# Head products on 64 array rows, two heads in turn, instead of zero-padded 128-row products

## The chip, the core and the metric

The kernel runs on one core of one Trainium2 chip. All numbers are 32-bit floats; the larger matrix products use pairs of a rounded and a remaining part ("hi" and "lo"), three products to one. The metric is the device time of one execution in microseconds (us).

## The reference

256 tokens of width 1024 go through two blocks, one after the other. Cut to what matters here:

```python
# first block: a mixer of two halves, then a layer of 32 experts
z = h @ w_in                                   # h: normalised, modulated x
y_a = gmlp_mixer(zu, zv, ...)
y_b = rwkv7_mixer(zr, ...)                     # 8 heads of 64 channels:
#   state = state * w[:, None, :] + (state @ a)[..., None] * b[:, None, :] + v[..., None] * k[:, None, :]
#   y_t   = state @ r
x = x + gate1 * (concatenate([y_a, y_b]) @ w_out)
x = rmsnorm(x + gate2 * hier_moe(...))
# second block: two layers
for i in range(2):
    q, k, v = heads(h @ w_qkv[i])              # 16 heads of 64 channels
    if i == 0:                                 # stick-breaking attention, s < t
        z = (q @ k.T) * 64 ** -0.5
        a = exp(log_sigmoid(z) + after)        # after: sum of log_sigmoid(-z) over s < j < t
    else:                                      # forgetting attention, s <= t
        a = softmax(z + cum_t - cum_s)
    x = x + gt_a * rmsnorm((a @ v) @ w_o[i])
    x = x + gt_f * rmsnorm(ffn(...))
```

## The kernel before, in words

A list scheduler decides the order of the instructions on each engine; every engine then runs its own list in order and waits on semaphores. All loads of weights are issued on SP's queue in program order. The stages follow each other: norm and gmlp and rwkv projections (to about 128 us of the profiled execution), the rwkv products (128 to about 200 us), the output projection, router and experts (to about 760 us), then layer 0 of the second block with stick-breaking attention (about 780 to 900 us), its feed-forward, layer 1 with forgetting attention, its feed-forward.

**The rwkv products.** The recurrence is computed in two chunks of 128 tokens. `Bt`, `Kt` (keys, scaled) and `AR` (what they are multiplied with, two kinds of 128 columns a chunk) hold channels on partitions: a pair `q` of heads fills 128 partitions, head `e` of the pair lies on `E2[e]`, rows 0 to 63 or 64 to 127. A product over one head's 64 channels is wanted. `BP` and `KP` are copies of `Bt` and `Kt` with one 128-row slab a head, in which the other head's rows are zero: POOL zeroes both at the kernel's start (L677, L678), ACT copies the head's 64 rows (L694, L699, 8 copies each), and TensorE multiplies all 128 rows (L738 for `BP`, L752 for `KP`). Each source line's matmul over 256 columns appears in the trace as two records, so the 16 matmuls of L738 are 32 records. DVE masks a head's first product into `NT` and `RB` (L741, L742), POOL makes `XT` of `NT` (L743, L744), and DVE transposes `XT` to `Y`, four heads' slabs at a time (L785). DVE masks a head's second product into `ma` (L755), and eight records a head multiply `ma` with `V` (L759, L760). Products of `Y` and `NT` (L776) start the inversion that follows, and quarters of modulation vectors (L184, on 32 array columns) are filled in between.

**Layer 0's scores.** `project` makes queries and keys of a pair of heads. ACT copies the keys into `kz`, one head at a time, the other head's rows zero (L1441, two copies of 64x256), and the queries into `kq` (L1444, one copy). POOL zeroes the two `kz` buffers at the block's start (L1296). `stick_scores` multiplies them (L1456 with 256 columns, L1457 with 128), head after head, into one PSUM bank a head. Layer 1 uses the same buffers: POOL zeroes `kq` (L1409), DVE writes a row of ones into `kz` (L1413).

```python
            for e in range(2):
                h = 2 * q + e
                r = AR[:, q].rearrange("p c x t -> p c (x t)")
                p = pmm()
                for c in range(2):
                    PE.matmul(p[:, 256 * c:256 * c + 256], BP[:, h, 128 * c:128 * c + 128], r[:, c, :], start=c == 0,
                              stop=c == 1, skip_group_check=True)
```

Of the kernel before, what the change touches and what calls it, by code (L numbers as in the profile page):

```python
# [11 lines left out]
F32 = mybir.dt.float32  # L12
# [8 lines left out]
D = 1024  # L21
# [4 lines left out]
BIG = 6                                                  # 8 KB slots beside the ring's  # L26
MORE = 2                                                 # and those that the experts add
QUAD = 4                                                 # the four experts after which crowded places have their turn
# of the experts' pieces of weights that are loaded ahead: those that go where later tiles lie, and the order of loading
EARLY = {4: "em", 5: "ay", 11: "oo", 17: "xg"}  # L30
ORDER = (0, 1, 2, 3, 6, 7, 8, 9, 10, 4, 5, 11, 12, 13, 14, 15, 16, 17)
# quarters of the modulation vectors emitted between other work
# [5 lines left out]
# row tiles of weights after which the products so far are emitted  # L38
ENDV = (1, 2, 3, 4, 6, 7)
ENDO = (0, 2, 3, 7)  # L40
# pieces of weights split ahead
# [3 lines left out]
ONACT = (1, 2, 3)                                        # row tiles of the first norm that ScalarE writes  # L45
# [3 lines left out]
# first columns of the parameters in their array  # L49
# [10 lines left out]
def block(ctx, tc, A, out, dbg=None):  # L60
# [7 lines left out]
    # 8 KB tiles of all phases; the experts' weights are staged in them too  # L68
# [5 lines left out]
    split = []                                           # the pool of the phase for parts of weights  # L74
# [12 lines left out]
    # ---------------------------------------------------------------- constants  # L87
# [5 lines left out]
    gt, ge = gte[:, 0, :], gte[:, 1, :]                  # [p, j]: j > p, j >= p  # L93
    DVE.tensor_scalar(gt, jp, 0.0, None, op0=OP.is_gt)
    DVE.tensor_scalar(ge, jp, 0.0, None, op0=OP.is_ge)
    sel = const.tile([128, 1], F32, name="sel")          # 1 at partitions 0, 32, 64, 96
# [4 lines left out]
    # ---------------------------------------------------------------- inputs  # L101
    par = const.tile([128, NPAR], F32, name="par")       # the parameters as columns
# [26 lines left out]
    # ---------------------------------------------------------------- weights  # L129
# [35 lines left out]
    # ---------------------------------------------------------------- c @ W rows  # L165
# [83 lines left out]
    # ---------------------------------------------------------------- rmsnorm pieces  # L249
# [1425 lines left out]
```

## Time and profile before

| What | Value |
|---|---|
| median of 3 runs | 1476.15 us (1474.22 to 1479.09) |
| span of the profiled execution, first to last instruction | 1477.1 us; the trace lists no time outside it |
| PE busy | 1375.0 us, 93% |
| DVE busy | 763.4 us, 52% |
| ACT busy | 572.5 us, 39% |
| POOL busy | 77.1 us, 5% |
| mean granted TensorE clock | 0.974 of full speed |

How to read what follows. A timeline row is the start in us, the length in us, engine, line, operation, output and inputs, shape, and how many records were joined (x); in brackets the idle time of the engine before it and what ended that. A row of groups gives the busy time in us and the mean in ns of one, then the idle time before. A row of windows gives the stretch, its length, and busy time with number of instructions for PE, weight loads (PEld), DVE, ACT and POOL, then granted clock (1.00 is 2.4 GHz, 0.50 is 1.2 GHz), DMA share and GB/s. A row of waits gives who waited for whom: total us, times, longest. The ends of PE's records are modelled, so starts are used.

### The profile page before, as it was taken

What the parts mean: (1) busy time and instruction counts of PE and PEld (TensorE: products, weight loads), DVE (VectorE), ACT (ScalarE), POOL (GpSimd) and SP (SyncE); (2) the same over time, 40 slices, a digit from 0 to 9 for tenths busy, and PEclk for the clock granted to TensorE, in tenths of its full rate; (3) what the DMA queues carried; (4) which work ended last, traced back from release to release, by engine and by line L of the source; (5) the groups of instructions that cost most, each with busy time, mean ns of one, the idle gap of its engine ahead of it and who ended that gap; (6) DMA issues with size and microseconds to landing.
All of it is one profiled execution on the core that took longest, in us unless ns stands there. A gap on an engine that the chain in (4) does not pass through costs nothing.

```text
span 1477.1 us, 24948 instructions
## 1 busy us (share of the span) xinstructions
PE 1375.0 (93%) x10350; PEld 1069.9 (72%) x10350; DVE 763.4 (52%) x1499; ACT 572.5 (39%) x1020; POOL 77.1 (5%) x77
## 2 busy tenths in 40 slices
PE   7989998799999988898979999999998999999997
PEld 5778877555545555454548876899997897799997
DVE  6648767321112112111136885788876575666665
ACT  3533014211111101011136774554556686654544
POOL 1003000000000000000010221100020001100000
PEclk9989999799999999999999998999999999999999
DMA  9825589699999999999996463787775434555540
GB/s 368 300 65 221 200 297 389 245 350 386 394 391 391 393 389 350 398 390 391 389 382 228 173 234 131 287 317 285 285 256 200 156 133 141 193 180 197 178 165 29
DMA packets 261575, 400.55 MB, mean 271 GB/s; under 512 B 6561, under 2 KB 215729, under 8 KB 261458
## 3 DMA queue, kind: packets, MB, share of 16 engines
q1 hardware_dynamic: 261458, 398.91, 75.0%
q8 instruction: 83, 1.36, 0.3%
q14 instruction: 34, 0.28, 0.1%
HBM read 397.82 MB, written 1.05 MB: 270 GB/s over the span
## 4 chain that ended last, share of the span: by engine, by line
PE 51%; DVE 3%; ACT 3%; DMA 2%; issue 1%; POOL 0%; POOLq 0%; DVEq 0%; SPq 0%; ACTq 0%
PE pmm L410 8%; PE pmm L411 7%; PE pmm L412 7%; PE pacc L410 5%; PE pacc L411 5%; PE pacc L412 5%; PE pmm L1191 4%; PE pmm L1214 3%; DMA wcols<-in_moe_w_up_dram 1%; PE pmm L184 1%; DMA wrows<-in_w_qkv_dram 1%; PE pmm L1162 1%; PE pmm L429 1%; PE pmm L1543 1%; PE pmm L360 1%
## 5 line engine op out<-in xcount | busy, mean ns | idle before, releaser
L410 PE MATMUL pmm<-hh,whi 128*128 128x256 f32 (+1 forms) x1040 | 295.2, 284 | 2.0 <-ACT whi L161 2.0
L412 PE MATMUL pmm<-hh,wlo 128*128 128x256 f32 (+1 forms) x1040 | 296.0, 285 | 0.2 <-DVE wlo L162 0.2
L411 PE MATMUL pmm<-hl,whi 128*128 128x256 f32 (+1 forms) x1040 | 294.6, 283 | 0.0
L1191 PE MATMUL pmm<-wcols,xg 128*64 128x256 f32 x2048 | 231.7, 380 | 6.3 <-DMA wcols<-in_moe_w_up_dram 6.3
L162 DVE TENSOR_TENSOR wlo<-wcols,whi 128x1024 fp32r<-128x1024 f32 (+1 forms) x130 | 168.5, 1301 | 97.2 <-ACT whi L161 96.8
L1191 PEld LDWEIGHTS pmm<-wcols,xg 128*64 128x64 f32 x2048 | 146.2, 137 | 85.8 <-DMA wcols<-in_moe_w_up_dram 8.9
L410 PEld LDWEIGHTS pmm<-hh,whi 128*128 128x128 f32 (+1 forms) x1040 | 196.8, 189 | 8.5 <-issue 3.6
L411 PEld LDWEIGHTS pmm<-hl,whi 128*128 128x128 f32 (+1 forms) x1040 | 196.0, 188 | 1.4
L412 PEld LDWEIGHTS pmm<-hh,wlo 128*128 128x128 f32 (+1 forms) x1040 | 196.3, 189 | 0.6 <-DVE wlo L162 0.5
L161 ACT ACTIVATE whi<-wcols 128x1024 fp32r<-128x1024 f32 (+1 forms) x130 | 136.2, 1053 | 118.0 <-PE pmm L411 91.5
L162 DVE TENSOR_TENSOR wlo<-wrows,whi 128x1024 fp32r<-128x1024 f32 x87 | 108.2, 1249 | 54.3 <-ACT whi L161 53.9
L1201 DVE TENSOR_TENSOR ay<-ay,pmm 128x512 f32<-128x512 f32 x16 | 11.0, 688 | 240.1 <-PE pmm L1191 226.4
L1214 PE MATMUL pmm<-wrows,em 128*64 128x512 f32 x512 | 124.6, 598 | 11.0 <-ACT em L1206 11.0
L161 ACT ACTIVATE whi<-wrows 128x1024 fp32r<-128x1024 f32 x87 | 91.7, 1062 | 91.0 <-PE pmm L411 46.8
L1214 PEld LDWEIGHTS pmm<-wrows,em 128*64 128x64 f32 x512 | 38.9, 136 | 75.2 <-issue 58.1
L411 PE MATMUL pacc<-wlo,ah 128*128 128x512 f32 x176 | 69.2, 393 | 0.0
L410 PE MATMUL pacc<-whi,ah 128*128 128x512 f32 x176 | 68.9, 391 | 0.0
L412 PE MATMUL pacc<-whi,al 128*128 128x512 f32 x176 | 68.6, 393 | 0.0
L1222 DVE SCALAR_TENSOR_TENSOR ay<-pmm,wsl,ga 128x512 f32<-128x512 f32 x32 | 24.0, 751 | 84.7 <-PE pmm L1214 82.7
L1198 ACT ACTIVATE ay<-pmm 128x512 f32<-128x512 f32 x16 | 9.6, 598 | 131.1 <-PE pmm L1191 131.1
L1206 ACT ACTIVATE em<-pmm 128x512 f32<-128x512 f32 x16 | 9.5, 597 | 123.4 <-PE pmm L1204 123.4
L1223 ACT ACTIVATE o<-ay 128x512 fp32r<-128x512 f32 x32 | 20.2, 632 | 80.2 <-DVE ay L1222 73.0
(521 smaller groups left out, 2215.2 us busy)
## 6 DMA issues: line engine op xcount, KB each, us to landing
wcols<-in_moe_w_gate_dram SPq DMA_DIRECT2D x64, 1024.0 KB, 12.0
wcols<-in_moe_w_up_dram SPq DMA_DIRECT2D x64, 1024.0 KB, 10.7
wrows<-in_moe_w_down_dram SPq DMA_DIRECT2D x64, 1024.0 KB, 10.7
wrows<-in_w_mod_dram SPq DMA_DIRECT2D x48, 1024.0 KB, 6.9
wcols<-in_w_ffn_gate_dram SPq DMA_DIRECT2D x22, 1024.0 KB, 5.3
wcols<-in_w_ffn_up_dram SPq DMA_DIRECT2D x22, 1024.0 KB, 7.5
wrows<-in_w_ffn_down_dram SPq DMA_DIRECT2D x22, 1024.0 KB, 5.1
wrows<-in_ada_w_dram SPq DMA_DIRECT2D x16, 1024.0 KB, 7.5
```

What stands on the lines that cost most here:

```text
L161: ACT.activation(hi, src, AF.Copy)
L162: (POOL if ahead else DVE).tensor_tensor(lo, src, hi.bitcast(F32), op=OP.subtract)
L184: PE.matmul(p[32 * g:32 * g + 32, 0:n].rearrange("p (a j) -> p a j", j=32), lhsT, groups(rhs)[:, g], start=first, stop=last, skip_group_ch ...
L360: PE.matmul(p, src[:, i, 128 * kt:128 * kt + 128], dg[i], start=True, stop=True)
L410: PE.matmul(p, a[0], b[0], start=first, stop=False, skip_group_check=True)
L411: PE.matmul(p, a[0], b[1], start=False, stop=False, skip_group_check=True)
L412: PE.matmul(p, a[1], b[0], start=False, stop=last, skip_group_check=True)
L429: PE.matmul(p[:, 128 * a:128 * a + 128], c[:, 4 * n + a:4 * n + a + 1].to_broadcast([128, 128]), ident, start=a == 0, stop=a == 3, skip_gr ...
L1191: PE.matmul(p[64 * a:64 * a + 64, 256 * n:256 * n + 256], xg[:, kt, lc(es[a])], wt[a][:, kt, :], start=n == 0 and kt == 0, stop=kt == KT - ...
L1214: PE.matmul(pd[n][64 * a:64 * a + 64, :], hT[:, f, 64 * a:64 * a + 64], wt[a][:, b, 512 * n:512 * n + 512], start=f == 0, stop=f == 3, ski ...
L1222: DVE.scalar_tensor_tensor(yf, pd[n], wsl, ga2[:, ns], op0=OP.mult, op1=OP.mult)
L1223: ACT.activation(oh[:, ns], yf, AF.Copy)
```

## The change

The two padded copies `BP` and `KP` go, with their memsets and their 16 ACT copies. A new function `of_pair` takes two PSUM banks and multiplies on the head's own 64 rows, the two heads in turn. In layer 0 the keys are copied in one piece for both heads, and the scores are taken on 64 rows, heads in turn. Layer 1 keeps its padded products, so the zeroing of `kz` moves to layer 1's setup, ahead of each `kq`. The arithmetic is the same but for the zeros. All comments of the kernel are also taken out, which shifts line numbers: L738 and L752 become L727, L741/742 L736/737, L743/744 L738/739, L755 L745, L759/760 L749/750, L785 L775, L1296 and L1409 L1398, L1413 L1402, L1456 and L1457 L1445.

```diff
-        BP, KP = b8h("BP"), b8h("KP")
-        POOL.memset(BP, 0.0)
-        POOL.memset(KP, 0.0)
...
-            for e in range(2):
-                ACT.activation(BP[E2[e], 2 * q + e, :], Bt[E2[e], q, :], AF.Copy)
...
-            for e in range(2):
-                ACT.activation(KP[E2[e], 2 * q + e, :], Kt[E2[e], q, :], AF.Copy)
...
+        def of_pair(q, src):
+
+            r = AR[:, q].rearrange("p c x t -> p c (x t)")
+            ps = [pmm(), pmm()]
+            for c in range(2):
+                for e in range(2):
+                    PE.matmul(ps[e][:, 256 * c:256 * c + 256], src[E2[e], q, 128 * c:128 * c + 128], r[E2[e], c, :],
+                              start=c == 0, stop=c == 1, skip_group_check=True)
+            return ps
...
-            for e in range(2):
+            for e, p in enumerate(of_pair(q, Bt)):
...
-        for t in kz:
-            POOL.memset(t, 0.0)
...
-                for t in kq:
+                for t in kz + kq:
                     POOL.memset(t, 0.0)
...
+                    if ly == 0:
+                        t = (kz if n == "k" else kq)[pq % 2][:, 0, :]
+                        ACT.activation(t, p[:, 0:S], AF.Copy, scale=1.0 if n == "k" else HD ** -0.5)
...
-                for e in range(2):
-                    PE.matmul(pz[e][:, 0:256], z1[:, e, 0:128], mv, start=True, stop=True, skip_group_check=True)
-                    PE.matmul(pz[e][:, 256:384], z1[:, e, 128:256], mv[:, 128:256], start=False, stop=True,
-                              skip_group_check=True)
+                for o, r, t in ((slice(0, 256), slice(0, 128), slice(0, 256)),
+                                (slice(256, 384), slice(128, 256), slice(128, 256))):
+                    for e in range(2):
+                        PE.matmul(pz[e][:, o], z1[E2[e], 0, r], mv[E2[e], 0, t], start=r.start == 0, stop=True,
+                                  skip_group_check=True)
```

DVE's list in the rwkv products, before, from the mask of the eighth head's first product on (`ma` is a masked second product, `Y<-XT` a transpose of four heads' slabs):

```order
L741 TENSOR_TENSOR NT<-pmm,gte 128x2x128
L742 TENSOR_TENSOR RB<-pmm,gte 128x2x128
L785 STREAM_TRANSPOSE Y<-XT 128x512
L755 TENSOR_TENSOR ma<-pmm,gte 128x512 x3
L785 STREAM_TRANSPOSE Y<-XT 128x512 x3
L755 TENSOR_TENSOR ma<-pmm,gte 128x512 x5
```

The same place of DVE's list in the changed kernel, from the sixth head's mask on:

```order
L736 TENSOR_TENSOR NT<-pmm,gte 128x2x128
L737 TENSOR_TENSOR RB<-pmm,gte 128x2x128
L775 STREAM_TRANSPOSE Y<-XT 128x512
L736 TENSOR_TENSOR NT<-pmm,gte 128x2x128
L737 TENSOR_TENSOR RB<-pmm,gte 128x2x128
L736 TENSOR_TENSOR NT<-pmm,gte 128x2x128
L737 TENSOR_TENSOR RB<-pmm,gte 128x2x128
L745 TENSOR_TENSOR ma<-pmm,gte 128x512 x2
L775 STREAM_TRANSPOSE Y<-XT 128x512 x2
L745 TENSOR_TENSOR ma<-pmm,gte 128x512 x2
L775 STREAM_TRANSPOSE Y<-XT 128x512
L745 TENSOR_TENSOR ma<-pmm,gte 128x512 x4
```

The first transpose moved ahead of the last two heads' masks, and the second ahead of the third `ma`.

TensorE's list around layer 0's score products, before, at the fourth pair of heads (`hi` and `lo` are the next products' factors, `lb` the weights of the pair before):

```order
L1543 MATMUL pmm<-lb,vs 64x256 x2
L1545 MATMUL pmm<-lb,vs 64x128 x2
L184 MATMUL pmm<-wrows,csil 32x256 x8
L1456 MATMUL pacc<-kq_6097,kz_6095 128x256
L1457 MATMUL pacc<-kq_6097,kz_6095 128x128
L1456 MATMUL pacc<-kq_6097,kz_6095 128x256
L1457 MATMUL pacc<-kq_6097,kz_6095 128x128
L1480 MATMUL pacc<-hi,lt 128x512
```

And in the changed kernel, at the fifth pair:

```order
L1531 MATMUL pmm<-lb,vs 64x256 x2
L1533 MATMUL pmm<-lb,vs 64x128 x2
L184 MATMUL pmm<-wrows,csil 32x256 x8
L1445 MATMUL pacc<-kq_6076,kz_6074 128x256 x2
L1445 MATMUL pacc<-kq_6076,kz_6074 128x128 x2
L1468 MATMUL pacc<-hi,lt 128x512
```

The two heads' products of one size now stand next to each other; what is ahead of them and behind them is the same. In five of the eight pairs L184 stands ahead of the scores, in three (the first, second and fourth) the projections do.

## Rows read from the trace of the kernel before

**Rows 1.** The page: the chain that ended last, by engine.

```profile
PE 51%; DVE 3%; ACT 3%; DMA 2%; issue 1%; POOL 0%; POOLq 0%; DVEq 0%; SPq 0%; ACTq 0%
```

**Rows 2.** Windows: end of the rwkv products, ten us of layer 0's attention.

```profile
142.00:152.00 10.00, 8.31 (x60) 7.28 (x58) 5.50 (x9) 0.17 (x1) 0.00 (x0) 1.00 0.00 0
841.00:851.00 10.00, 10.00 (x89) 8.78 (x88) 8.13 (x16) 7.77 (x13) 2.08 (x1) 1.00 0.76 281
```

**Rows 3.** Groups by line and form, 0 to 480 us.

```profile
L785 DVE STREAM_TRANSPOSE Y<-XT 128x512 f32<-128x512 f32 x20 | 13.4, 691 | 3.4 <-POOL XT L744 3.3
L738 PE MATMUL pmm<-AR,BP 128*128 128x256 f32 x32 | 7.1, 379 | 0.0
L743 POOL TENSOR_TENSOR XT<-NT,offT 128x256 f32<-128x256 f32 x8 | 5.8, 728 | 124.0 <-DVE NT L741 124.0
L694 ACT ACTIVATE BP<-Bt 64x256 f32<-64x256 f32 x8 | 3.3, 418 | 4.4 <-DVE Bt L692 4.3
```

**Rows 4.** Timeline of the rwkv products.

```profile
129.84 0.73 POOL L743 TENSOR_TENSOR XT<-NT,offT 128x256 f32<-128x256 f32 x1 [123.99 <-DVE NT L741]
...
141.09 0.73 POOL L744 TENSOR_TENSOR XT<-XT,ident 128x256 f32<-128x256 f32 x1
...
144.38 0.43 PE L759 MATMUL pacc<-V,ma 128*128 128x64 f32 x2 [1.69 <-DVE ma L755]
...
146.22 1.51 PE L752 MATMUL pmm<-AR,KP 128*128 128x256 f32 x6
...
152.89 0.42 PE L184 MATMUL pacc<-wrows,par 128*32 128x256 f32 x4
```

**Rows 5.** Timeline: a pair's score products in layer 0.

```profile
811.35 0.70 PE L1456 MATMUL pacc<-kq,kz 128*128 128x256 f32 x2
...
812.68 0.36 PE L412 MATMUL pmm<-hh,wlo 128*128 128x256 f32 x1
```

**Rows 6.** Timeline: products on 64 and 32 array columns, then on 128.

```profile
826.10 0.65 PE L1543 MATMUL pmm<-lb,vs 128*64 128x256 f32 x4
...
826.90 1.07 PE L184 MATMUL pmm<-wrows,csil 128*32 128x256 f32 x16
...
827.90 0.39 PE L410 MATMUL pmm<-hh,whi 128*128 128x256 f32 x1
...
828.12 0.28 PE L411 MATMUL pmm<-hl,whi 128*128 128x256 f32 x1
...
828.25 0.28 PE L412 MATMUL pmm<-hh,wlo 128*128 128x256 f32 x1
```

**Rows 7.** Timeline of the norm ahead of layer 0.

```profile
766.05 3.26 DVE L1280 TENSOR_SCALAR lt<-jp 128x128 fp32r<-128x128 f32 x1
...
768.23 0.99 POOL L1296 MEMSET kz<- 128x512 f32 x2
768.31 1.07 DVE L1282 CAST one<-ones 128x128 fp32r<-128x128 f32 x1
...
771.80 1.19 PE L360 MATMUL pmm<-dg,tf 128*128 128x128 f32 x4 [7.54 <-DVE dg L1265]
```

**Rows 8.** Timeline: the last pair of layer 0.

```profile
880.36 0.53 POOL L1409 MEMSET kq<- 128x512 f32 x1 [1.97 <-PE pacc L1457]
...
884.42 2.34 POOL L162 TENSOR_TENSOR hilo<-wcols,hilo 128x1024 fp32r<-128x1024 f32 x1 [3.54 <-ACT hilo L161]
884.48 2.57 DVE L1469 TENSOR_TENSOR gm<-gm,gte 128x256 f32<-128x256 f32 x1
...
886.97 0.41 DVE L1470 TENSOR_TENSOR lb<-lb,mask 128x256 f32<-128x256 f32 x1
```

**Rows 9.** Windows: a long and a short stretch at half clock.

```profile
256.30:273.40 17.10, 8.07 (x38) 7.85 (x38) 11.61 (x45) 3.68 (x7) 4.68 (x2) 0.50 0.69 230
...
925.30:928.70 3.40, 3.32 (x16) 3.05 (x16) 1.25 (x3) 2.19 (x5) 0.64 (x1) 0.50 1.00 408
```

**Rows 10.** PE's waits over the whole run.

```profile
PE pmm L381 <- ACT ga L224: 1.9, 1, 1.9
```

More of the change, by code (lines that the diff above doesn't have):

```diff
@@ L673, in block @@
         Bt, Kt, km = qt("Bt"), qt("Kt"), qt("km")
-        b8h = lambda n: b8(n).rearrange("p (h c) t -> p h (c t)", h=8)
-        BP, KP = b8h("BP"), b8h("KP")
-        POOL.memset(BP, 0.0)
-        POOL.memset(KP, 0.0)
         E2 = [slice(0, 64), slice(64, 128)]
@@ L730, in block @@
         two = lambda m: m[:, None, :].to_broadcast([128, 2, 128])
+        def of_pair(q, src):
[6 more added lines that the diff above has]
+            return ps
         for q in range(4):
             fill(FILL_A[0])
-            for e in range(2):
+            for e, p in enumerate(of_pair(q, Bt)):
                 h = 2 * q + e
-                r = AR[:, q].rearrange("p c x t -> p c (x t)")
-                p = pmm()
-                for c in range(2):
-                    PE.matmul(p[:, 256 * c:256 * c + 256], BP[:, h, 128 * c:128 * c + 128], r[:, c, :], start=c == 0,
-                              stop=c == 1, skip_group_check=True)
                 p4 = p.rearrange("p (c x t) -> p c x t", c=2, x=2)
@@ L746, in block @@
             fill(FILL_A[1])
-            for e in range(2):
+            for e, p in enumerate(of_pair(q, Kt)):
                 h = 2 * q + e
-                r = AR[:, q].rearrange("p c x t -> p c (x t)")
-                p = pmm()
-                for c in range(2):
-                    PE.matmul(p[:, 256 * c:256 * c + 256], KP[:, h, 128 * c:128 * c + 128], r[:, c, :], start=c == 0,
-                              stop=c == 1, skip_group_check=True)
                 ma = pool.tile([128, 2, 2, 128], F32, name="ma", tag="tmp2", bufs=3)
@@ L1438, in project @@
                         mm3(p[:, 0:S], (hi[:, kt, :], lo[:, kt, :]), (hh[:, kt, :], hl[:, kt, :]), kt == 0, kt == KT - 1)
-                    if (n == "k") == (ly == 0):
+                    if ly == 0:
+                        t = (kz if n == "k" else kq)[pq % 2][:, 0, :]
+                        ACT.activation(t, p[:, 0:S], AF.Copy, scale=1.0 if n == "k" else HD ** -0.5)
+                    elif n == "q":
                         for e in range(2):
                             ACT.activation(kz[pq % 2][E2[e], e, :], p[E2[e], 0:S], AF.Copy)
-                    elif ly == 0:
-                        mv = kq[pq % 2][:, 0, :]
-                        ACT.activation(mv, p[:, 0:S], AF.Copy, scale=HD ** -0.5)
                     else:
-                        mv = kq[pq % 2]
                         for e in range(2):
-                            ACT.activation(mv[E2[e], e, :], p[E2[e], 0:S], AF.Copy, scale=HD ** -0.5)
-                            ACT.activation(mv[XR[e], e, :], ncr[XR[e], pq, :], AF.Copy)
-                return kz[pq % 2], mv
+                            ACT.activation(kq[pq % 2][E2[e], e, :], p[E2[e], 0:S], AF.Copy, scale=HD ** -0.5)
+                            ACT.activation(kq[pq % 2][XR[e], e, :], ncr[XR[e], pq, :], AF.Copy)
+                return kz[pq % 2], kq[pq % 2]
             def stick_scores(pq, z1, mv):
                 pz = [pacc(), pacc()]
-                for e in range(2):
-                    PE.matmul(pz[e][:, 0:256], z1[:, e, 0:128], mv, start=True, stop=True, skip_group_check=True)
-                    PE.matmul(pz[e][:, 256:384], z1[:, e, 128:256], mv[:, 128:256], start=False, stop=True,
-                              skip_group_check=True)
+                for o, r, t in ((slice(0, 256), slice(0, 128), slice(0, 256)),
[3 more added lines that the diff above has]
+                                  skip_group_check=True)
                 lb, lo, hi = wide("lb"), wide("lo", F32R), wide("hi", F32R)
```

## The prediction

> **What bounds the kernel now.** I read the chain that ended last first: TensorE holds 51% of it and no other engine over 3% [rows 1], so the question at each place that the change touches is whether TensorE works or waits there. The windows answer it. In layer 0's attention TensorE is busy 10.00 of 10 us, DVE 8.13 and ACT 7.77 [rows 2]: less TensorE work shortens the stage nearly one for one. At the end of the rwkv products it is busy 8.31 of 10 us [rows 2]; the 1.69 us that is missing is one wait, for DVE's third masked product after a transpose [rows 4]. The groups show what stands behind that: DVE's transpose of `XT` waits 3.3 us for POOL [rows 3], and POOL's row of 16 operations of 0.73 us runs without a pause from 129.84 to 141.82 us [rows 3, 4]. So POOL, not the padded products, sets the first half of that stage.
>
> **The padding's upkeep.** Two memsets on POOL at the kernel's start and 16 ACT copies of 0.42 us (8 of L694, and 8 of L699 like them) [rows 3] go. I cost both at nothing: POOL does nothing that is waited for until 129.84 us [rows 4], and the copies lie where TensorE is filled by the projections, with ACT idle 4.3 us ahead of them for DVE alone [rows 3]. If that cover were thin, the last copy is what could matter, at most 0.42 us.
>
> **The rwkv products.** The 32 records of L738 (and as many of L752) are 379 ns each by their modelled ends [rows 3]; side by side they could take half of TensorE's time. For L738 that is worth nothing: POOL starts when the first head's mask is there, and then needs 8 x 2 x 0.73 = 11.7 us whatever TensorE does. A pair's two heads now end together, so the first mask starts no earlier. Behind POOL's end the lists decide. Before, three `ma` stand ahead of the transpose that waits for POOL, so five are left; now two do, and six are left: one head's eight records with `V` more for TensorE, (146.22 - 144.38) / 2 = 0.9 us, since two heads' records stand between these rows [rows 4], **+0.9**. One transpose of 0.69 us [rows 3] fewer stands between POOL's end and the first of them, **-0.6**. One of six products of `Y` and `NT` moves behind L184, two records half as long as those of L738, **-0.2**. The second products: five were left (ten records of 0.22 us, 7.1 / 32, 2.2 us); now seven are left, four of them in pairs and three alone, five slots if a pair runs side by side, again 2.2 us, **0**. And the array's shape changes back and forth for four groups between the products with `V`, eight changes at 0.1 us each (below), **+0.8**. The sum is **+0.9 us** for the start of L184 at 152.89 [rows 4]. Bounds: -0.5 with no price for the changes and everything in half the time; +2.5 without overlap (0.9 for four records more) and nearly twice the price.
>
> **Layer 0's scores.** A pair's products take 1.33 us from their first record to the next projection [rows 5]. If the heads run side by side, half goes: 0.66 us a pair, 5.3 us for eight. The trace of before has no two products on different rows and the same columns, so the overlap is bounded from the nearest rows: four records of L1543 on 64 columns each take 0.65 us together, sixteen of L184 on 32 columns 1.07 us [rows 6], which is two and four at a time (one at a time, sixteen of 0.22 us would be 3.5 us). I take full overlap, the other end is none. The price of the new shape: the last group of L184 starts 0.38 us (the length of such a record [rows 3]) ahead of its end at 827.97, at 827.59, and the next product 0.31 us later, where the four groups follow each other at 0.23; and the second product behind it comes 0.22 us later instead of 0.13 (827.90, 828.12, 828.25) [rows 6]. So leaving a shape costs about 0.2 us. Entering is already paid in the five pairs in which L184 stands ahead of the scores, and is new in three, for which I take 0.1 us each. Together 8 x 0.2 + 3 x 0.1 = 1.9 us, and -5.3 + 1.9 = -3.4. As DVE has 8.13 of 10 us of its own work there [rows 2], I let a little of it be lost: **-3.0 us**. Bounds: -5.3 with no price for the shapes, +1.9 with the price and no overlap. The one copy instead of two for the keys is off TensorE's path: the products behind L184 start 0.31 us after it with or without a wait for `kz`.
>
> The Trainium skill, "TensorEngine Tiling (Array Packing)", section Key Properties, says that changing the tiling mode drains the engine, and that tiles of one mode work in parallel; its Overview gives up to 2x for a contraction of 64. By the 2x alone this part would be -5.3 us; the drain speaks against the change, has no price there, and the rows of before agree with it (0.31 us where 0.23 is the rule). No run so far shows row tiles.
>
> **The norm ahead of layer 0.** TensorE is idle 7.54 us until 771.80 for a chain on DVE [rows 7]. In it the cast of `one` takes 1.07 us, from 768.31 to 769.38, and POOL's two memsets of `kz` lie over it until 769.22 [rows 7]; DVE's next operations wait for it. The memsets move away. If they hold the cast, it ends soon after its start, up to 0.9 us earlier; if the cast is slow by itself, nothing. I take **-0.8 us**, because the operation ahead of it also lasted 3.26 us, to just where the memsets ran.
>
> The Trainium skill, "SBUF — State Buffer", section Who interferes with whom, says that DVE's casts and its operations with one scalar operand can need a pair of ports that GpSimd shares, and that whoever is first locks the other out for the whole operation. By it this term is -0.9 us; without it the row would allow 0. The trace agrees with it so far: 3.26 us for 128x128 elements.
>
> **Layer 1's setup.** POOL zeroes `kz` as well, two memsets of 0.53 us ahead of those of `kq` [rows 8], and DVE's rows of ones now wait for them. Behind the second of these waits stand DVE's operations of the last pair, on which TensorE waits. POOL's next work starts only at 884.42 [rows 8], so it isn't late. I take **+0.1 us**, between 0 and +0.3.
>
> **Sum.** -3.0 - 0.8 + 0.9 + 0.1 = -2.8 us. The profiled execution spans 1477.1 us, 0.95 above the median of the runs; so 1474.3 by its own time, and **1473.4** by the median. What is gained before 200 us is carried on, because the experts' loads follow the router. The ends add up to -6.7 and +4.7 us. A change of 0.3%, 4.4 us, is about what can be told from none here.
>
> **Rivals.**
>
> *The heads don't run side by side.* Then scores cost +1.9, the rwkv products +2.5, the rest -0.7: +3.7 us, 1479.9. For it speaks that no rows of this trace show row tiles; against it, that column tiles do overlap. Chance 0.13.
>
> *The clock falls in the rwkv products: slower.* TensorE will wait twice there, by the new DVE order: about 2 us for the seventh and eighth heads' masks behind the first transpose, and about 2.4 us until the third `ma`. Before it was one wait of 1.69 us without a fall. Elsewhere a wait of 1.9 us was followed by 3.4 us at half clock, from 925.30 on [rows 9, 10]. A stretch of 3.4 us costs at most 1.7 us, which gives 1475.1; one like that of 17.1 us [rows 9] costs up to 8.5 and gives 1481.9. It decides from 7.2 us on, 14 us of TensorE's work at 1.2 GHz. Chance of any fall 0.3, of one beyond that point 0.08.
>
> *A collision dissolves: faster.* In the last pair DVE's `gm` takes 2.57 us where the same kind of operation takes 0.41, because POOL's `hilo` began 0.06 us ahead of it [rows 8]. TensorE waits for it. Were DVE first, 2.1 us go: -4.9, 1471.3. Both hang on the same ACT chain, so a shift of one against the other is unlikely: 0.1. A full -5.3 for the scores has the same effect on the verdict: -5.1, 1471.1, chance 0.15.
>
> **How the numbers follow.** The forecast as summed, with or without a short fall of the clock: 0.54, nearly all within 0.3%. No overlap 0.13, on the slow side of it, a third beyond. Long fall 0.08: slower. The two faster cases 0.25. That makes faster 0.26, same 0.61, slower 0.13. The range reaches from 1469.5, near the sum of the good ends, to 1479.9, the case without overlap.
>
> **What would show it.** L1445: the two heads' records a few ns apart, and a pair's products below 1.0 us. The cast of `one` well under 0.5 us, and TensorE's first product of the norm 0.8 us sooner after POOL's `hilo`. POOL's chain of `XT` still 12 us long; L184 23 to 25.5 us after that chain's start. A granted clock of 0.5 between 137 and 155 us would show the second rival. The prediction is wrong if products on 64 rows start as far apart as those on 128, or if a shape's change costs much more than 0.2 us.

## The result and the profile after

| | before | after |
|---|---|---|
| median of 4 runs each, on one chip | 1477.53 us (1474.22 to 1479.09) | 1490.45 us (1489.19 to 1490.79) |
| ratio, with its 95% interval | | 1.0081 [1.0065, 1.0097] |
| span of the profiled execution | 1477.1 us | 1488.8 us |
| mean granted TensorE clock | 0.974 | 0.969 |
| rwkv products: first product to the start of the last mask `W` | 56.7 us | 69.7 us |
| layer 0's scores: first to last record | 68.7 us | 71.1 us |

The changed kernel is 0.8% slower; the prediction said 0.2% faster, and the time lies outside its range. The chain that ended last, by engine, is led by TensorE as in [rows 1], with a smaller share of the span, so it doesn't say where the time went:

```profile
PE 37%; DVE 2%; ACT 2%; issue 1%; POOL 0%; POOLq 0%; DVEq 0%; DMA 0%; ACTq 0%
```

TensorE still holds most of it, and no other engine over 2%. The windows say where. Three stretches of the changed kernel's rwkv products, and the ten us of its layer 0 that answer to [rows 2]:

```profile
128.00:137.00 9.00, 6.61 (x43) 4.37 (x41) 5.41 (x16) 0.96 (x2) 6.73 (x10) 1.00 0.40 154
137.00:168.00 31.00, 30.60 (x133) 23.20 (x134) 9.60 (x18) 2.07 (x4) 4.59 (x7) 0.50 0.04 9
168.00:180.00 12.00, 12.00 (x124) 10.95 (x122) 10.38 (x18) 0.39 (x1) 0.00 (x0) 1.00 0.74 265
...
841.00:851.00 10.00, 8.26 (x56) 7.93 (x58) 7.05 (x16) 5.15 (x8) 1.69 (x1) 0.83 0.26 88
```

And the kernel before in the second of these stretches:

```profile
137.00:168.00 31.00, 29.31 (x264) 25.89 (x264) 19.40 (x33) 2.45 (x5) 4.58 (x7) 1.00 0.36 124
```

TensorE is as busy in both, but it finishes 133 instructions instead of 264: the granted clock is 0.50, from 137.22 us on and for 30.7 us. A busy share alone would have hidden this. The timeline shows what stands ahead of the fall:

```profile
128.20 4.94 PE L727 MATMUL pmm<-AR,Bt 64*128 64x256 f32 x31
...
129.88 0.73 POOL L738 TENSOR_TENSOR XT<-NT,offT 128x256 f32<-128x256 f32 x1 [127.54 <-DVE NT L736]
...
137.40 1.85 PE L727 MATMUL pmm<-AR,Kt 64*128 64x256 f32 x4 [2.72 <-DVE RB L737]
...
141.10 0.72 POOL L739 TENSOR_TENSOR XT<-XT,ident 128x256 f32<-128x256 f32 x1
```

POOL's chain of `XT` runs as in [rows 4], 129.88 to 141.82 us. The last of the first products starts at 133.0 us instead of 134.9. After the first few of the second products TensorE stands idle for 2.72 us, until DVE's masks, which stand behind its first transpose, free a bank; 0.2 us before the end of this wait the clock falls. The masks that write `W`, which end the stage, start at 163.4 to 197.9 us instead of 151.5 to 184.9. First the rows of before, then those of the changed kernel (ns of the shortest, the median and the longest, then the first and the last start in us):

```profile
L738 PE MATMUL pmm<-AR,BP x32: 379/379/382, 128.2 to 134.9; 128*128 128x256 f32 x32
L792 DVE TENSOR_TENSOR W<-pmm,off x16: 654/692/693, 151.5 to 184.9; 128x512 f32<-128x512 f32 x16
```

```profile
L727 PE MATMUL pmm<-AR,Bt x32: 376/376/480, 128.2 to 133.0; 64*128 64x256 f32 x32
L782 DVE TENSOR_TENSOR W<-pmm,off x16: 654/692/692, 163.4 to 197.9; 128x512 f32<-128x512 f32 x16
```

From the first to the last of these starts, 128.2 to 197.9 us, the stage takes 69.7 us, 13.0 more than before. The rest of the span's difference of 11.7 us: -2.2 from there on to layer 0's norm and its wait (experts included), +2.4 in layer 0's scores, +0.2 behind them, -1.7 afterwards, where two short falls of the clock of before (at 1239 and 1273 us, 3.4 us each) don't occur and a third (at 1133 us before) is 3.4 us longer.

The norm, with the rows that answer to [rows 7]:

```profile
777.72 2.35 DVE L1270 TENSOR_SCALAR lt<-jp 128x128 fp32r<-128x128 f32 x1
779.98 0.22 DVE L1272 CAST one<-ones 128x128 fp32r<-128x128 f32 x1
...
782.62 1.19 PE L360 MATMUL pmm<-dg,tf 128*128 128x128 f32 x4 [6.68 <-DVE dg L1255]
```

The cast takes 0.22 instead of 1.07 us, and TensorE waits 6.68 instead of 7.54 us.

Layer 0's scores at 839 us:

```profile
838.96 0.92 PE L1445 MATMUL pacc<-kq,kz 64*128 64x256 f32 x8
839.81 1.22 DVE L162 TENSOR_TENSOR wlo<-wcols,whi 128x1024 fp32r<-128x1024 f32 x1
839.88 0.50 PE L1468 MATMUL pacc<-hi,lt 128*128 128x512 f32 x1
...
839.91 2.78 POOL L1460 TENSOR_TENSOR lo<-gm,hi 128x768 fp32r<-128x768 f32 x1 [6.79 <-PE pacc L1445]
...
842.74 0.50 PE L1468 MATMUL pacc<-lo,lt 128*128 128x512 f32 x1 [2.00 <-POOL lo L1460]
```

A pair's products take 0.92 us here (838.96 to 839.88), and 0.85 in each of the other seven pairs, instead of the 1.33 of [rows 5]: the two heads do run side by side. But TensorE then waits 2.00 us for POOL's `lo`. Its waits for `lo` in the whole stage:

```profile
PE pacc L1468 <- POOL lo L1460: 3.5, 3, 2.0
```

Before, these were one wait of 0.3 us. About 1 us behind the one of 2.00 us the clock falls again, for 3.4 us from 843.78 on.

### The profile page after: what moved, and what is told of

It is laid out like the page before. It is cut to its first block, busy times and chain, and to the rows that moved or that the text cites. A ratio compares the mean times of both kernels' runs of the same rounds, so it can differ in the third digit from the quotient of the medians.

```text
span 1488.8 us, 24919 instructions
## 1 busy us (share of the span) xinstructions
PE 1379.0 (93%) x10350; PEld 1070.6 (72%) x10350; DVE 757.8 (51%) x1499; ACT 562.0 (38%) x996; POOL 75.5 (5%) x75
## 5 line engine op out<-in xcount | busy, mean ns | idle before, releaser
L162 DVE TENSOR_TENSOR wlo<-wcols,whi 128x1024 fp32r<-128x1024 f32 (+1 forms) x130 | 165.2, 1275 | 102.0 <-ACT whi L161 101.7
L1181 PEld LDWEIGHTS pmm<-wcols,xg 128*64 128x64 f32 x2048 | 149.5, 137 | 85.2 <-DMA wcols<-in_moe_w_up_dram 10.3
```

The costliest lines, as they stand in the source:

```text
L162: (POOL if ahead else DVE).tensor_tensor(lo, src, hi.bitcast(F32), op=OP.subtract)
L1181: PE.matmul(p[64 * a:64 * a + 64, 256 * n:256 * n + 256], xg[:, kt, lc(es[a])], wt[a][:, kt, :], start=n == 0 and kt == 0, stop=kt == KT - ...
```

## The experiments

Three theories stood against each other. **The clock**: TensorE's work, thinner on 64 rows (less of it in the same stretch), with the new waits lets the granted clock fall, and the half clock is the loss. **The order**: the scheduler's new lists lose the time whatever the products' rows are. **The rows**: products on 64 rows are slower in themselves, by their changes of shape or because the heads don't overlap. The expectations ask further what brings a fall: A, TensorE's wait; B1, the products on 64 rows; B2, the time that the overlap frees; C in them is a loss in layer 0. The table gives each run's ratio to the kernel before on the same chip (95% interval), the length of the rwkv stage as above, how long the clock was at half in that stage, and TensorE's longest wait there. Clock and waits are read from one profiled execution of each kernel. That the long falls recur is seen in the times: every execution of rwkv_only, rw_fill_wait and pairs_only took longer than every one of the kernel before on the same chip (for the closest, pairs_only, 1483.76 us or more against 1480.53 or less).

| Run | ratio | stage, us | half clock, us | wait, us |
|---|---|---|---|---|
| rwkv_only | 1.0098 [1.0078, 1.0119] | 69.8 | 30.7 | 2.71 |
| attn_only | 1.0000 [0.9989, 1.0011] | 56.7 | none | 1.68 |
| rw_ma_first | 1.0014 [0.9997, 1.0032] | 59.5 | 10.2 | 0.78 |
| pad_ma_first | 0.9996 [0.9980, 1.0012] | 55.2 | none | none |
| pad_early | 1.0009 [0.9996, 1.0021] | 56.8 | none | 1.34 |
| rw_ma_first_twice | 1.0048 [1.0024, 1.0073] | 60.1 | none | 0.78 |
| rw_early_junk | 1.0063 [1.0039, 1.0087] | 66.2 | none | none |
| attn_lo_dve | 0.9972 [0.9957, 0.9987] | 56.7 | none | 1.66 |
| pad_wait | 1.0011 [1.0000, 1.0022] | 57.7 | none | 2.42 |
| rw_fill_wait | 1.0070 [1.0049, 1.0092] | 66.0 | 17.1 | 1.73 |
| best1 | 0.9968 [0.9953, 0.9983] | 55.2 | none | none |
| pad_lo_dve | 0.9988 [0.9973, 1.0003] | 56.7 | none | 1.66 |
| pairs_only | 1.0061 [1.0045, 1.0077] | 66.0 | 27.3 | 2.72 |
| rw_pairs | 0.9974 [0.9961, 0.9987] | 50.8 | none | none |
| pad_half | 0.9939 [0.9915, 0.9963] | 48.1 | none | 0.22 |
| best2 | 0.9932 [0.9920, 0.9945] | 50.8 | none | none |

**Each half alone.** rwkv_only makes the change in the rwkv products alone, attn_only in layer 0's scores and the zeroing of `kz` alone. Of the diff above, the first takes these lines, the second leaves them out:

```diff
-        BP, KP = b8h("BP"), b8h("KP")
...
+        def of_pair(q, src):
```

> Only the rwkv half of the change: products on 64 rows, no padded copies; layer 0's scores and the zeroing of kz are as before. Theory A (TensorE waits 2.7 us behind DVE's early transpose, the clock falls there and stays at 1.2 GHz for about 30 us): granted clock 0.5 from about 137 to about 168 us, L184 behind the products at about 163 us instead of 152.9, the whole 10 to 14 us slower than before. Theory C (the loss is in layer 0's attention): within 3 us of before.

> Only the second half of the change: scores on 64 rows, one copy of the keys, kz zeroed in layer 1's setup; the rwkv products are padded as before. Theory A: no fall of the clock in the rwkv products, the whole between 3 us faster and 3 us slower than before; the cast of one ahead of layer 0 takes 0.2 us instead of 1.07. Theory C: 5 us or more slower, from TensorE's waits for POOL's lo in layer 0.

All of the loss is in the first half, 13.4 us by the medians (1491.11 against 1477.71). The second half gives nothing: 1477.44 us. In attn_only TensorE also waits 2.00 us for `lo`, between the same products as in the changed kernel, and no fall follows; the clock stays at 1.00 from 776 to 884 us:

```profile
830.82 0.50 PE L1476 MATMUL pacc<-lo,lt 128*128 128x512 f32 x1 [2.00 <-POOL lo L1468]
```

So such a wait between such products doesn't always bring a fall, and the short one in layer 0 of the changed kernel stays unexplained.

**DVE's order.** rw_ma_first and pad_ma_first hold DVE's transposes behind the eighth `ma`, so that TensorE doesn't wait for them; the first on 64 rows, the second with padded products. pad_early is the opposite: padded products with DVE's list in the changed kernel's order.

```diff
+        mas = []
...
+                mas.append(DVE.tensor_tensor(ma, p.rearrange("p (c x t) -> p c x t", c=2, x=2),
...
+        with tc.issue_after(mas[7].ins):
+            for g in range(4):
+                turn_blocks(g)
```

```diff
+            if q == 2:
+                turn_after(0, last)
...
+                if h == 1:
+                    turn_after(1, last)
+                    turn_after(2, last)
+                if h == 3:
+                    turn_after(3, last)
```

> As rwkv_only, but DVE's four transposes are held behind the eighth ma, so that TensorE has products with V while POOL works. Theory A (the wait brings the fall): no wait over 1.5 us, full clock throughout, L184 at 145 to 149 us, the whole 3 to 8 us faster than before. Theory B (products on 64 rows bring the clock down whatever stands around them): granted clock 0.5 in the products all the same, L184 at 155 us or later, the whole 3 us or more slower than before.

> As before, with padded products on 128 rows, but with the same hold of DVE's transposes behind the eighth ma. By theories A and B alike full clock; L184 at 146 to 149 us against 152.9, the whole 3 to 6 us faster than before. Beside rw_ma_first it shows what the 64 rows are worth once DVE's order is the same: theory A 0 to 2 us for the 64 rows, theory B a loss with them.

> Padded products on 128 rows as before, layer 0 as before, but DVE's list is held to the changed kernel's order: the first transpose behind the sixth head's masks, the next two behind the second ma. Theory A (the wait alone brings the fall): a wait of about 2 us or more of TensorE between 133 and 145 us, granted clock 0.5 behind it, 5 to 14 us slower than before. Theory B1 (products on 64 rows bring it) and B2 (the time that the overlap frees on TensorE brings it, whatever fills the lists): full clock, 0 to 3 us slower than before from the order alone.

The order by itself is out: with padded products pad_early takes 56.8 us for the stage, before 56.7. Its longest wait was only 1.34 us, so it doesn't test the wait. pad_ma_first was to be 3 to 6 us faster than before and is 0.7 us faster by the medians, 1.5 in the stage. With the transposes held back, ten of the 13 us return; but the clock of rw_ma_first still falls, which theory A didn't expect, later and for 10.2 us:

```profile
127.00:145.00 18.00, 16.73 (x110) 12.35 (x107) 9.17 (x22) 0.46 (x1) 11.32 (x16) 1.00 0.17 68
145.00:155.00 10.00, 9.22 (x56) 6.09 (x56) 4.29 (x8) 2.06 (x4) 0.00 (x0) 0.50 0.09 14
```

No wait ahead of it is longer than 0.50 us; the one of 0.78 in the table lies within the fall. So a long wait isn't needed for a fall, and this run alone doesn't say what is. Its executions lie between 1476.64 and 1488.95 us, so the fall may not be as long in each. pad_ma_first in the second of these stretches:

```profile
145.00:155.00 10.00, 10.00 (x98) 8.53 (x97) 7.49 (x14) 2.06 (x4) 0.00 (x0) 1.00 0.35 113
```

**More work on TensorE.** rw_ma_first_twice makes each product on 64 rows twice. rw_early_junk takes the changed kernel's order of DVE's list and puts a product on 128 rows, which is overwritten, ahead of each on 64.

```diff
+            for _ in range(2):
                 for c in range(2):
                     for e in range(2):
```

```diff
+            for e in range(2):
+                for c in range(2):
+                    PE.matmul(ps[e][:, 256 * c:256 * c + 256], src[:, q, 128 * c:128 * c + 128], r[:, c, :],
+                              start=c == 0, stop=c == 1, skip_group_check=True)
```

> As rw_ma_first (64 rows, transposes behind the eighth ma), but every product on 64 rows is made twice, the second overwriting the first, so that TensorE is as long in them as with padding and the shapes and the order stay. Theory B2 (freed time): no fall between 128 and 160 us, L184 at 149 to 152 us, 1 to 4 us faster than rw_ma_first though it computes more. Theory B1 (64 rows): clock 0.5 from about 145 us as in rw_ma_first, or sooner, and no faster than it.

> As rwkv_only with the same DVE order, but ahead of each product on 64 rows the same bank gets a product on all 128 rows that is then overwritten: one and a half times the padded kernel's work in these products. Theories A and B2: the waits shrink below 2 us, no fall or one of under 7 us, 6 to 12 us faster than rwkv_only though it computes more. Theory B1: the fall stays about 30 us long and the time is that of rwkv_only or above.

Both keep the full clock through the stage. Twice the products in the same order, at full clock:

```profile
145.00:160.00 15.00, 13.87 (x125) 11.26 (x126) 7.65 (x14) 2.06 (x4) 0.00 (x0) 1.00 0.16 45
```

It has waits like those of rw_ma_first (three of 0.35 us and one of 0.78), on 64 rows and with as many changes of shape, and takes 60.1 us, hardly more than that run with half the products and a fall (59.5). This speaks for thin work as the cause, and against the 64 rows as such. It is no test of what the clock costs, since the added work takes time itself: rw_early_junk, without a fall and without a wait, still needs 66.2 us. Neither gained what theory B2 forecast: rw_ma_first_twice is 7.0 us slower than before by the medians, where rw_ma_first is 0.9 slower, and rw_early_junk is 9.1 slower, where rwkv_only is 13.4. A part of rw_ma_first_twice's loss lies outside the stage: its stretch at half clock in the router lasts 23.9 us, where [rows 9] has 17.1.

**The wait alone, and the wait filled.** pad_wait is pad_early with two more transposes ahead of the third `ma`, so that TensorE waits about as long as in the changed kernel, on padded products. rw_fill_wait is rwkv_only's order with eight products on 128 rows, which nobody reads, in the first wait.

```diff
-                    turn_after(2, last)
+                    for _ in range(3):
+                        turn_after(2, last)
```

```diff
+            if q == 0:
+                for _ in range(8):
+                    with behind(tail[0]):
+                        tail[:] = [PE.matmul(pm[0][:, 0:256], Bt[:, 0, 0:128], AR[:, 0].rearrange("p c x t -> p c (x t)")[:, 0, :],
+                                             start=True, stop=True, skip_group_check=True)]
```

> As pad_early (padded products, DVE's list in the changed kernel's order), with two more transposes of the same slabs on DVE behind the third one, so that TensorE's wait grows from 1.34 us to 2.7 or more: the wait of the changed kernel without its 64 rows. If a wait of this length is enough to bring the clock down: granted clock 0.5 from about 144 us on, L184 31 us or more after the first product, 4 us or more slower than before. If it takes less work in the products as well: full clock, L184 about 27 us after the first product, 1 to 3 us slower.

> As rwkv_only with the same DVE order and each product made once on 64 rows, but eight products on all 128 rows, which nobody reads, fill TensorE's wait ahead of the first products with V (about 3.5 us). If TensorE's idle stretch there brings the fall: no fall or a short one, L184 24 to 28 us after the first product instead of 35.5, 8 to 13 us faster than rwkv_only though it computes more. If the sparse work behind it is enough: the fall comes all the same, 10 us or more slower than before.

pad_wait's timeline and its windows behind the wait:

```profile
146.13 0.43 PE L784 MATMUL pacc<-V,ma 128*128 128x64 f32 x2 [2.42 <-DVE ma L774]
```

```profile
139.00:150.00 11.00, 8.58 (x59) 7.74 (x58) 7.33 (x12) 0.00 (x0) 3.52 (x5) 1.00 0.00 0
150.00:160.00 10.00, 10.00 (x103) 8.90 (x103) 4.83 (x9) 2.06 (x4) 0.00 (x0) 1.00 0.34 112
```

A wait of 2.42 us between padded products doesn't bring the clock down. It is 0.30 us shorter than the changed kernel's, and stands 9 us later, so it isn't the same wait; but it is three times the longest of rw_ma_first, which fell. In rw_fill_wait the fall is not gone but moved, and shorter: from 145.13 us on, 17.1 us long, 2.7 us behind the end of the next wait in the list:

```profile
142.43 0.43 PE L784 MATMUL pacc<-V,ma 128*128 128x64 f32 x2 [1.73 <-DVE ma L775]
```

A wait of 1.69 us between padded products ([rows 4]) brings none. Filling one hole shortens the fall but doesn't remove it, while the work behind the hole stays thin and has another.

**The products kept together.** In rw_ma_first the two products of a pair come apart: the scheduler puts lone ones between the products with `V`, as their banks come free. rw_pairs issues both of a pair behind the last product with `V` of the pair whose banks they take, which leaves 6 changes of shape instead of 14, the one ahead of the first products included. pairs_only has this without the hold on the transposes.

```diff
+        kps = [of_pair(q, Kt) for q in range(2)]
...
-            for e, p in enumerate(of_pair(q, Kt)):
+            for e, p in enumerate(kps.pop(0)):
...
+            if q < 2:
+                with tc.issue_after(v.ins):
+                    kps.append(of_pair(q + 2, Kt))
```

> As rw_ma_first (64 rows, transposes behind the eighth ma), but a pair's second products are kept together, so that the array changes its shape 6 times among the products with V instead of 14. If the changes of shape and the thin stretches around them bring the fall: no fall between 128 and 160 us, the last W mask 53 to 56 us after the first product against 59.5, 3 to 6 us faster than rw_ma_first. If the freed time alone brings it: clock 0.5 again from about 145 us, 57 us or more.

> As rwkv_only, with one edit: a pair's second products are kept together behind the products with V of the pair two before, so that the array changes its shape 6 times among these instead of 10; DVE's list stays free, with its early transposes and TensorE's waits. If the scattered products alone bring the fall: full clock, the last W mask under 58 us after the first product, within 3 us of before. If the wait of 2.7 us is needed and enough with 64 rows: clock 0.5 behind it, 62 us or more, 6 us or more slower than before.

The windows of rw_pairs over 28 us, and of pairs_only:

```profile
134.00:162.00 28.00, 28.00 (x272) 24.66 (x269) 20.93 (x36) 2.45 (x5) 6.24 (x9) 1.00 0.43 149
```

```profile
134.00:162.00 28.00, 26.50 (x130) 21.34 (x131) 9.92 (x18) 2.06 (x4) 5.60 (x8) 0.51 0.05 15
```

The two kernels differ in where DVE's transposes stand, and with that in the wait of 2.72 us, which only pairs_only has. Its clock falls, and it takes 66.0 us; rw_pairs is never idle there, has the full clock and takes 50.8. First the wait of pairs_only, a window that ends just before its end, and its masks that write `W`, then those of rw_pairs:

```profile
135.50 2.71 PE L727 MATMUL pmm<-AR,Kt 64*128 64x256 f32 x8 [2.72 <-DVE RB L737]
```

```profile
134.40:135.40 1.00, 0.00 (x0) 0.00 (x0) 1.00 (x4) 0.00 (x0) 0.92 (x2) 0.50 0.00 0
```

```profile
L786 DVE TENSOR_TENSOR W<-pmm,off x16: 650/691/692, 162.0 to 192.3; 128x512 f32<-128x512 f32 x16
```

```profile
L788 DVE TENSOR_TENSOR W<-pmm,off x16: 650/691/692, 147.4 to 177.7; 128x512 f32<-128x512 f32 x16
```

The wait began at 132.78 us, and the clock fell at 134.35, while TensorE was still idle: 1.6 us of this wait stood ahead of the fall, less than the 2.42 us in pad_wait that brought none. Of the 15.2 us between the two kernels the order by itself is worth 1.6 on padded products (pad_early's 56.8 to pad_ma_first's 55.2), which leaves 13.6 for the fall and its wait; half of 27.3 us, the most that the half clock can cost, is 13.7. With neither the wait nor the scattering, the products on 64 rows are 5.9 us better than before and 4.4 better than padded ones in the same order. Of the 5.9 us the whole run shows 3.7 by the medians.

**Freed time on 128 rows.** pad_half is pad_ma_first with the products of each pair's first head alone; the second head's masks read the same bank. It leaves out half of the products, so its output is not the kernel's; TensorE gets the same relief as on 64 rows, but all its work is on 128 rows.

```diff
-                p = pmm()
-                for c in range(2):
+                p = p if e else pmm()
+                for c in range(0 if e else 2):
```

> As pad_ma_first (128 rows, no change of shape), but only the first head of each pair gets its two products; the second head is masked from the same bank. It leaves out half of these products, so its output is not the kernel's. TensorE is freed of the same time as by the overlap, on 128 rows. If the freed time alone brings the fall: clock 0.5 from some point between 135 and 155 us, the last W mask 57 us or more after the first product. If it takes the 64 rows and their changes of shape: full clock, 53 to 55.2 us.

No fall, and 48.1 us. The stretch behind the first products:

```profile
134.00:140.00 6.00, 5.78 (x39) 4.87 (x38) 5.41 (x12) 0.00 (x0) 5.69 (x9) 1.00 0.02 4
```

So freed time by itself doesn't bring the clock down, as it doesn't in rw_pairs. No run has both on 128 rows, the freed time and a long wait.

**Layer 0's `lo`.** attn_lo_dve is attn_only, and pad_lo_dve the kernel before, with `lo` on DVE instead of POOL.

```diff
-                POOL.tensor_tensor(lo, lm, hi.bitcast(F32), op=OP.subtract)
+                DVE.tensor_tensor(lo, lm, hi.bitcast(F32), op=OP.subtract)
```

> As attn_only (rwkv products padded as before, scores on 64 rows), but layer 0's lo is subtracted on DVE instead of POOL. In attn_only TensorE gained about 0.35 us a pair and waited for POOL's lo instead, 2.0 us at once. If that wait is where the scores' gain went: no wait for lo over 1 us, DVE's wlo no longer held up, 3 to 6 us faster than before. If DVE becomes the bound: within 2 us of before or slower.

> The kernel before with one edit: layer 0's lo is subtracted on DVE instead of POOL; scores padded as before. If the 64 rows are what attn_lo_dve gained by, once lo doesn't hold TensorE up: within 1.5 us of before. If DVE's freedom from POOL is the gain: 3 us or more faster than before.

The windows of attn_only and of attn_lo_dve over most of the stage:

```profile
812.00:872.00 60.00, 56.31 (x489) 48.10 (x489) 46.66 (x88) 41.98 (x68) 14.08 (x8) 1.00 0.55 190
```

```profile
812.00:872.00 60.00, 59.25 (x521) 51.73 (x520) 52.61 (x109) 44.31 (x71) 0.99 (x2) 1.00 0.60 211
```

With `lo` on DVE, TensorE is busy 59.25 of 60 us instead of 56.31, although DVE has 6 us more to do. The scores take 65.6 us, against 69.4 in attn_only, 67.9 in pad_lo_dve and 68.7 before. So the scores on 64 rows are worth 2.3 us (67.9 - 65.6) where POOL doesn't hold them up, and cost 0.7 where it does; `lo` on DVE with padded scores is worth 0.7. By the whole times pad_lo_dve doesn't decide its question: it is 0.12% faster than before, 1.8 us, between the 1.5 and the 3 that would have told.

**Together.** best1 takes the padded rwkv products of pad_ma_first with the change in layer 0 and `lo` on DVE. best2 is the whole change with the held transposes, the pairs kept together and `lo` on DVE, the diffs shown above.

> Put together: rwkv products padded as before with DVE's transposes behind the eighth ma, layer 0's scores on 64 rows, one copy of the keys, kz zeroed in layer 1's setup, lo on DVE. By the sum of pad_ma_first (up to 1.5 us at the end of the products) and attn_lo_dve (4.2 us): 4 to 7 us faster than before, faster than the before kernel and than the changed one.

> The whole change with two mends: in the rwkv products DVE's transposes stand behind the eighth ma and a pair's second products are kept together (rw_pairs), and layer 0's lo is subtracted on DVE (attn_lo_dve). By the sum of the two, 3.7 and 4.5 us between medians: 7 to 9 us faster than before, 19 to 21 us faster than the change as it stands.

best2 takes 1467.82 us (1467.15 to 1470.24), 0.68% less than before and some 22 us less than the changed kernel; best1 1473.93 us, 4.6 less than before, as forecast. By the medians best2 gains 10.2 us where the sum of rw_pairs and attn_lo_dve is 8.2. One difference is seen in the traces, and what sets it isn't shown: in the router rw_pairs has 23.9 us at half clock, best2 17.1 in two pieces.

## Why the prediction was wrong, point by point

**The step that failed** is the rwkv term of the sum, +0.9 us at full clock, where the stage lost 13.0; and with it the chance of the second rival, *the clock falls in the rwkv products*, which would have given the sign: "Chance of any fall 0.3, of one beyond that point 0.08." Its place was right, between 137 and 155 us, and so was the kind of wait; its weight and its size were wrong. The wait was put at "about 2 us" and was 2.72 (the second wait, put at 2.4, didn't come); the stretch at half clock was sized by the longest one known, 17.1 us, and lasted 30.7. What stood against the rival was that a wait of 1.69 us before brought no fall. That compared waits alone. The runs show that a wait of 2.42 us does nothing between padded products (pad_wait) and that 64 rows do nothing without wait or scattering (rw_pairs). The falls in this stage came where thinner work and a wait stood together, or thinner work in scattered lone products with several short waits (rw_ma_first). Both came with the change.

The price follows from the same runs: half clock for 30.7 us costs at most 15.4 us, and the stage lost 13.0. Without the fall it would have taken at least 69.7 - 15.4 = 54.3 us; that is a bound, and no run has this order without a fall and without other work. Shown is that the fall goes with a longer stage in five kernels (changed, rwkv_only, pairs_only, rw_fill_wait, rw_ma_first) and that moving DVE's transposes in pairs_only, which takes away its wait, takes away both. Why the clock stays down for some 30 us, why rw_ma_first fell without a long wait, and why attn_only did not fall behind its 2.00 us stays open.

The Trainium skill, "TensorE: Matmul & The Clock Gate", section HAM oscillation — how this bites in real kernels, tells of a kernel with little work between its waits for data, whose products start at half clock behind every one of them. The runs here agree in that the falls in the rwkv products came where little work and waits stood together; a wait by itself, 2.42 us in pad_wait, did nothing.

**The rwkv sum of +0.9 us.** POOL's chain was as long as forecast, and DVE's new order costs nothing (pad_early), as its terms +0.9, -0.6 and -0.2 nearly cancel. That the relief of TensorE is worth nothing in this stage holds for the order that the sum took as given, not for another: with the transposes held back, rw_pairs gains 4.4 us on pad_ma_first. The price of 0.1 us for a change of shape was too small. In rw_ma_first, at full clock, a lone head's two records with the changes there and back:

```profile
134.63 0.39 PE L751 MATMUL pacc<-V,ma 128*128 128x64 f32 x2
134.95 0.70 PE L728 MATMUL pmm<-AR,Kt 64*128 64x256 f32 x2
135.58 0.43 PE L750 MATMUL pacc<-V,ma 128*128 128x64 f32 x2
135.85 0.39 PE L751 MATMUL pacc<-V,ma 128*128 128x64 f32 x2
136.07 0.39 PE L750 MATMUL pacc<-V,ma 128*128 128x64 f32 x2
```

The rows of two records with `V` follow each other 0.22 us apart (135.85 to 136.07). The lone head's row starts 0.32 us after the row with `V` ahead, the next row with `V` 0.63 us later, and the one behind it 0.27 us after that: 1.22 us where two records of 0.21 and two steps of 0.22 make 0.86, so 0.18 us for each of the two changes.

**The scores, -3.0 us.** The products' part was right: side by side, 0.85 to 0.92 us a pair where under 1.0 was forecast. The step "less TensorE work shortens the stage nearly one for one" failed: POOL's `lo`, of 1.8 to 2.8 us, became what is waited for, +0.7 us without the clock (attn_only) and +2.4 with the fall behind that wait. I had looked at DVE's and ACT's load there, not at POOL's chain, which has a low busy share but stands between two products.

**The norm, -0.8 us.** Right: -0.85 for the cast, -0.86 for TensorE's wait.

**Layer 1's setup, +0.1 us.** The memsets cost no wait that the trace shows: DVE isn't idle ahead of its rows of ones. TensorE's first wait in the last pair still grew, from 2.12 to 2.98 us, in attn_only too, for a reason that the sum didn't have. DVE's `gc`, which took 0.16 us before, now begins 0.30 us behind POOL's last `lo` but one and lasts to its end; TensorE also reaches this wait sooner, as the scores ahead of it are 0.5 us shorter. How the 0.86 us divide between the two isn't shown. First the `gc` of before, then the changed kernel:

```profile
872.22 0.16 DVE L1560 SCALAR_TENSOR_TENSOR gc<-modc,par 128x8 f32<-128x8 f32 x1
```

```profile
891.12 2.07 POOL L1460 TENSOR_TENSOR lo<-gm,hi 128x768 fp32r<-128x768 f32 x1 [6.67 <-ACT hi L1459]
891.42 1.79 DVE L1548 SCALAR_TENSOR_TENSOR gc<-modc,par 128x8 f32<-128x8 f32 x1
...
897.64 0.65 PE L1531 MATMUL pmm<-lb,vs 128*64 128x256 f32 x4 [2.98 <-ACT lb L1478]
...
898.62 3.73 POOL L162 TENSOR_TENSOR hilo<-wcols,hilo 128x1024 fp32r<-128x1024 f32 x1 [3.94 <-ACT hilo L161]
898.70 0.40 DVE L1457 TENSOR_TENSOR gm<-gm,gte 128x256 f32<-128x256 f32 x1
...
900.77 0.80 PE L1468 MATMUL pacc<-hi,lt 128*128 128x512 f32 x1 [0.39 <-ACT hi L1459]
...
904.17 0.80 PE L1468 MATMUL pacc<-lo,lt 128*128 128x512 f32 x1 [1.33 <-POOL lo L1460]
```

The third rival, the dissolved collision, came true in its way, but not to its gain. `gm` takes 0.40 us and `hilo` is held, 3.73 instead of the 2.34 of [rows 8]; TensorE's wait for `hi` behind it falls from 2.73 us to 0.39. The held `hilo` puts off POOL's last `lo`, though, and TensorE waits 1.33 us for that, where it didn't before. With the 0.86 the three nearly cancel: this is in the +0.2 us behind the scores.

**The first rival**, heads that don't run side by side, is false: the two heads' records start 6 to 7 ns apart.

## What to carry to other kernels

Products on part of the array's rows, two at a time, take less of TensorE's time (0.85 us a pair of heads here instead of 1.33), but what they leave is thin: ask of each wait between them what it does to the granted clock, keep the products of one shape together, and move the waiting work behind them before you count the gain. When a stage gets shorter on the engine that bounds it, look for the engine whose chain is late next by its place in the chain and not by its busy share, as POOL's `lo` here. And read the granted clock beside the busy share: 30.60 of 31 us busy was half the work.

## What the runs showed of the hardware

- Two products on different 64 rows and the same columns start 6 to 7 ns apart (128.202 and 128.209 us), and the next two follow after 209 ns, where the padded records of before started one every 0.22 us (32 of L738 from 128.2 to 134.9). A pair of heads so takes the time of one. In the second half of the first products the starts are less even, up to 0.45 us apart.
- A fall of the clock lasted 30.7 (changed), 27.3 (pairs_only), 17.1 (rw_fill_wait, with eight products more) and 10.2 us (rw_ma_first) in four orders of the rwkv products, and 3.4 us behind a wait in layer 0. In pairs_only it began while TensorE had been idle for 1.6 us; in pad_wait 2.42 us idle brought none.
- POOL and DVE hold each other up in either direction. At 839.81 us DVE's `wlo` began 0.10 us ahead of POOL's `lo`, which took 2.78 us (2.07 by the median of its eight); at 891.12 us POOL's `lo` began 0.30 us ahead of DVE's `gc`, which took 1.79 us instead of 0.16; at 898.62 us POOL's `hilo` began 0.08 us ahead of DVE's `gm`, and yet `hilo` was the one held. The Trainium skill, "SBUF — State Buffer", section Who interferes with whom, says that whoever issues first locks the other out. The first two cases agree with it; in the third the start in the profile doesn't tell who was first.
